# Second attention: scores and projections share one ring of five PSUM banks

## The chip, the cores and the metric
One core of a Trainium2 chip runs the whole kernel. The metric is the device time of one execution in microseconds (us). TensorE multiplies and transposes into PSUM, which has eight banks of 128 x 512 float32; VectorE and ScalarE read PSUM; GpSimd (POOL) works in SBUF; all DMAs are issued on SyncE's queue (SP).

## The reference
A decoder trunk of two layers over 2048 positions of width 1024. Each layer adds `W_out(mixer(RMSNorm(x)) * silu(gate))` to x. Layer 0 mixes by stick-breaking attention, 16 heads of 64. Layer 1, which the change touches, is multi-head latent attention with 8 heads:
```
q = rms_norm(rms_norm(q_lat) @ w_uq)          # per head 128 plain + 64 rotary
k = rms_norm(concat(kv_lat' @ w_ukv[:128], k_pe));  v = kv_lat' @ w_ukv[128:]
q, k = rope on their last 64
o = causal softmax(q k^T / sqrt(192)) v
x = x + (o * silu(gate)) @ w_out
```

## The kernel before
The program is written as a list of operations for a planner (`Sched`) inside the kernel. It gives each operation an estimated duration and issues, step by step, the one that can start first on its engine; among those that can start within 60 ns of each other, the one written first goes. So the order on each engine is fixed when the kernel is built. A matrix product of float32 quality is three products of a high and a low part (`HLS`), each a matmul of the type float32r.

A tile belongs to a ring, named by its tag, of so many buffers. A tile takes a buffer when the first operation on it is issued. A ring's queue holds its tiles in the order in which they are written. The tile at the head may take any free buffer; a tile behind the head may take one only where the ring has a `spare` number, and that many free buffers must be left over.

All PSUM comes from one pool `ps` (`bank`): three banks for `z`, two for `t`, one for `av`, two for `pj` with one spare.

The second attention goes through 32 stages (head h, group j of 512 positions). `proj1(n+1)` is written ahead of `attn1(n)`.
- `proj1` loads the latents (`ckv`, `cqt`), projects keys and values (`wukv`, two banks, the first stage `z`, the others `pj`), for every even head projects the queries of two heads (`wuq`, four banks), normalises, turns `qs`, `kn` and `kq` through one bank each, and copies half of the rotary operand `qpt` by DMA. It uses `pj`; in the first two stages also `z` and `t`.
- `attn1` makes the scores, 4(j+1) tiles `z` of five matmuls each. VectorE takes the maximum, ScalarE the exponent into `s` (a ring of 21), which releases the bank. POOL scales `s`. TensorE turns `s` through `t`, ScalarE and VectorE split it into `pt`, and three matmuls for each block add it into `av`.

Before this stage the gate of layer 1 runs through `t` and `pj` in turn (line 872). After it `out_proj` forms 16 tiles of the output, each with two accumulators, from `pj` and `z` in turn.

Of the kernel before, what the change touches and what calls it, by code (L numbers as in the profile page):

```python
# [11 lines left out]
F32 = mybir.dt.float32  # L12
# [5 lines left out]
PSUM = bass.MemoryType.PSUM  # L18
DRAM = bass.MemoryType.DRAM

P = 128
D = 1024
KD = D // P
EPS = 1e-6
NEG = -1.0e30
G = 512
# [358 lines left out]
def trunk(ctx: ExitStack, tc: tile.TileContext, x, w0, wo0, g0, g1, wlat, wgate, gqa, gkva,  # L385
# [3 lines left out]
    NT = S // P  # L389
    NG = S // G  # L390
    ctx.enter_context(tc.manual_schedule())
    sched = Sched()
# [6 lines left out]
    ps = sched.pool(lambda: tc.tile_pool(name="ps", bufs=1, space=PSUM))  # L399
    dram = ctx.enter_context(tc.tile_pool(name="dram", bufs=1, space=DRAM))  # L400

    def scratch(shape, name):
        return Buf(shape, tile=dram.tile(shape, F32, name=name))

    def bank(tag):
        bufs, spare = {"z": (3, None), "t": (2, 1), "av": (1, None), "pj": (2, 1)}[tag]
        return ps.tile([P, G], F32, tag, bufs, spare)
# [283 lines left out]
    yts = {}  # L691
# [24 lines left out]
            sched.spread(late, len(sched.ops), len(sched.ops), len(sched.ops) + 60)  # L716


    def out_proj(i, yt, xt, after=None, order=range(KD), dst=None):

        acc = [bank("pj" if i % 2 == 0 else "z") for _ in range(2)]

        def mul(ns, k):
            for a, b in HLS:
                for n in ns:
                    y = yt[k][a] if isinstance(yt[k], list) else yt[k][:, a, :]
                    w = wo[k][b][n] if isinstance(wo[k], list) else wo[k][:, b, n * G:(n + 1) * G]
                    C.mm(acc[n], y[:, i * P:(i + 1) * P], w, k == order[0] and a == 0 and b == 0,
                         k == order[-1] and a == 1)

        for ns in ((0,), (1,)) if dst is not None else ((0, 1),):
            for k in order:
                with sched.group():
                    mul(ns, k)
                if after:
                    after(k)
            for n in ns:
                cs = slice(n * G, (n + 1) * G)
                C.tt("dve", xt[:, cs], acc[n], xt[:, cs], ALU.add)
                if dst is not None:  # L740
                    C.dma(dst[:, cs], xt[:, cs], 256)
# [50 lines left out]
    for j in range(NG):  # L792
        done = []
        for i in range(4):
            t = 4 * j + i
# [128 lines left out]
    def proj1(n):  # L924
        h, j = stages[n]
        if j == 0:
            load_wh(h)
        load_c(n)
        wq, wkv = wh["q"], wh["kv"]
        kn = pa1.tile([P, 4, P], F32, "kn")  # L930
        vv = pk1.tile([P, 4, 2, P], F32R, "vv1", 6)
        ssk = pa1.tile([P, 4], F32, "ssk", 2)
        ckv = wh["ckv"]
        for i2 in range(0, 4, 2):
            acc = bank("z" if n == 0 else "pj")
            for i in range(i2, i2 + 2):
                t = slice(i * P, (i + 1) * P)
                o = 256 * (i - i2)
                with sched.group():
                    for n_, (a, b) in enumerate(HLS):  # L940
                        C.mm(acc[:, o:o + 256], ckv[:, a, t], wkv[:, b, :], n_ == 0, n_ == 2, 256)
                j1 = pa1.tile([P, QK1], BF16, "j1", 2)
                C.act(j1[:, 0:P], acc[:, o:o + P], AF.Square, P, accum=ssk[:, i:i + 1])
            av_ = acc.all().rearrange("p (i e d) -> p i e d", i=2, e=2)
            C.copy("dve", kn[:, i2:i2 + 2, :], av_[:, :, 0, :], 256)
            split(vv[:, i2:i2 + 2, 0, :], vv[:, i2:i2 + 2, 1, :], av_[:, :, 1, :], 256)
        C.tt("pool", ssk, ssk, kss[:, 4 * j:4 * j + 4], ALU.add, 4)
        rk4 = rstd(pa1, ssk, 4, QK1, "ak")
        for i in range(4):
            C.ts("dve", kn[:, i, :], kn[:, i, :], rk4[:, i:i + 1], 1.0, n=P)  # L950
        if h % 2 == 0:
            cqt = wh["cq"]
            ssq = pa1.tile([P, 8], F32, "ssq", 2)
            for i in range(4):
                acc = bank("z" if i % 2 == n else "pj")
                t = slice(i * P, (i + 1) * P)
                with sched.group():
                    for n_, (m, (a, b)) in enumerate([(m, ab) for m in range(2) for ab in HLS]):
                        C.mm(acc[:, 0:2 * QK1], cqt[:, m, a, t], wq[:, b, m, :], n_ == 0, n_ == 5, 2 * QK1)
                for e in range(2):  # L960
                    if i == 0:
                        qs1[h + e, j] = [pw1.tile([P, 4, QK1], F32, f"qs{e}", 1 + 3 * e)]
                    es = slice(e * QK1, (e + 1) * QK1)
                    j1 = pa1.tile([P, QK1], BF16, "j1", 2)
                    C.act(j1, acc[:, es], AF.Square, QK1, accum=ssq[:, 4 * e + i:4 * e + i + 1])
                    C.act(qs1[h + e, j][0][:, i, :], acc[:, es], AF.Copy, QK1)
            rq8 = rstd(pa1, ssq, 8, QK1, "aq", 5)
            for e in range(2):
                qs1[h + e, j].append(rq8[:, 4 * e:4 * e + 4])
        qs, rq4 = qs1[h, j]  # L970
        for i in range(4):
            C.ts("dve", qs[:, i, :], qs[:, i, :], rq4[:, i:i + 1], ISQ, n=QK1)
        js = slice(4 * j, 4 * j + 4)
        t1, t2 = rope(pa1, qs[:, :, P:QK1], cq[:, js, :], sq[:, js, :], 4, "rq")
        kq = pa1.tile([P, 4, 2, 64], F32, "kq")
        C.tt("pool", kq[:, :, 0, :], kper[:, js, :], rk4.all().unsqueeze(2).broadcast_to([P, 4, 64]), ALU.mult, 256)
        C.tt("pool", kq[:, :, 1, :], t1, t2, ALU.add, 256)
        qn = pk1.tile([P, 2, G], F32R, "qn", 2)
        qpt = pk1.tile([P, 2, G], F32R, "qpt", 2)
        knt = pk1.tile([P, 2, G], F32R, "knt", 5)  # L980
        kpt = pk1.tile([P, G], F32R, "kpt", 5)

        def tr(f):
            tb = bank("t" if n < 2 else "pj")
            with sched.group():
                for i in range(4):
                    C.turn(tb[:, i * P:(i + 1) * P], f(i), ident)
            return tb

        tb = tr(lambda i: qs[:, i, 0:P])  # L990
        split(qn[:, 0, :], qn[:, 1, :], tb)
        tb = tr(lambda i: kn[:, i, :])
        split(knt[:, 0, :], knt[:, 1, :], tb, gain=gqk)
        tb = tr(lambda i: kq[:, i].rearrange("p a b -> p (a b)"))
        split(kpt[0:64, :], kpt[64:128, :], tb[0:64, :])
        split(qpt[64:128, 0, :], qpt[64:128, 1, :], tb[64:128, :])
        C.dma(qpt[0:64].bitcast(F32), qpt[64:128].bitcast(F32), 256)
        kv1[h, j] = (knt, kpt, vv)
        cur1[h, j] = (qn, qpt)

    def attn1(h, j):
# [3 lines left out]
        for rt in range(4):  # L1005
# [3 lines left out]
            for g in range(j + 1):  # L1009
                knt, kpt, _ = kv1[h, g]  # L1010
                diag = g == j
                W = (rt + 1) * P if diag else G
                z = bank("z")
                with sched.group():
                    C.mm(z[:, :W], qn[:, 0, t], knt[:, 0, :W], True, False, W)
                    C.mm(z[:, :W], qn[:, 0, t], knt[:, 1, :W], False, False, W)
                    C.mm(z[:, :W], qn[:, 1, t], knt[:, 0, :W], False, False, W)
                    C.mm(z[:, :W], qpt[:, 0, t], kpt[:, :W], False, False, W)
                    C.mm(z[:, :W], qpt[:, 1, t], kpt[:, :W], False, True, W)
                if diag:  # L1020
                    C.mask_min(z[:, :W], z[:, :W], mask1[:, G - W:G], nm[:, g:g + 1], W)
                else:
                    C.reduce(nm[:, g:g + 1], z[:, :W], ALU.max, W, negate=True)
                s = pa1.tile([P, G], F32, "s", SB)
                C.act(s[:, :W], z[:, :W], AF.Exp, W, bias=nm[:, g:g + 1], scale=-1.0 if diag else 1.0,
                      accum=sm[:, g:g + 1])
                st[rt, g] = (s, W)
# [12 lines left out]
                C.ts(eng, s[:, :W], s[:, :W], c[:, g:g + 1] if j else 1.0, ri[:, 1:2], n=W)  # L1040
        g1t = pa1.tile([P, G], F32, "g1t", 2)
        C.dma(g1t, g1_d[j, h], 256)
        av = bank("av")
        for g in range(j + 1):
            vv = kv1[h, g][2]
            for c in range(4):
                r0 = c if g == j else 0
                t0 = r0 * P
                tb = bank("z" if last and c % 2 else "t")
                with sched.group():  # L1050
                    for rt in range(r0, 4):
                        C.turn(tb[:, rt * P:(rt + 1) * P], st[rt, g][0][:, c * P:(c + 1) * P], ident)
# [21 lines left out]
    yts = {}  # L1074
# [16 lines left out]
    for j in range(NG):  # L1091
        for i in range(4):
            t = 4 * j + i
            xt = pfo.tile([P, D], F32, "xr", 5)
            C.dma(xt, x1_d[t], 512)

            def ahead(k):
                if i == 1 and j + 1 < NG:
                    yts[j + 1, k] = load_y(pfo, y1_d, j + 1, k, "y", 12)

            end = out[t * P:(t + 1) * P, :]
            out_proj(i, [yts[j, k] for k in range(KD)], xt, ahead, dst=end if t == NT - 1 else None)
            if t < NT - 1:
                C.dma(end, xt, 512)

# [56 lines left out]
```

## Time and profile before
| what | us |
|---|---|
| median of 3 runs | 3049.11 (3048.87 to 3050.19) |
| the profiled execution, its own time | 3047.57 |
| its span | 3045.8 |
| TensorE busy | 2971.5 (98%) |
| VectorE busy | 2024.4 (66%) |
| ScalarE busy | 1864.7 (61%) |
| POOL busy | 1493.3 (49%) |

Busy time of TensorE counts each matmul to a modelled end, and one begins before the one ahead of it has ended. So gaps are read from the start times, and from the waits that the profile names.

### The profile page before, as it was taken

To read this page: it belongs to the slowest core of one execution; us is meant where nothing else is said; L and a number is where in the kernel's file an instruction comes from. 1 tells how busy PE (TensorE), PEld (TensorE's weight loads), DVE (VectorE), ACT (ScalarE), POOL (GpSimd) and SP (SyncE) were. 2 spreads that over 40 slices of the span, in tenths; PEclk is the share of its full clock that TensorE was granted. 3 is DMA by queue.
4 is the path that set the end of the run, shared out by engine and by line. 5 is a ranking of instruction groups with operands and counts; after the bars stand their busy time and mean duration, and the time that the engine had idled before them with its cause. 6 is when DMAs were issued, how large, how long until landed. Compare 5 with 4: busy or idle time off the path is not lost.

```text
span 3045.8 us, 48516 instructions
## 1 busy us (share of the span) xinstructions
PE 2971.5 (98%) x15728; PEld 2482.4 (82%) x15728; DVE 2024.4 (66%) x3553; ACT 1864.7 (61%) x4635; POOL 1493.3 (49%) x2931
## 2 busy tenths in 40 slices
PE   8999999999999999999999999999999999999999
PEld 6788888888888888888778888878888888888787
DVE  5787787878878788796953221147778777778511
ACT  5686776867768687786852132157776776777400
POOL 5574765756557475664652121136455555455200
PEclk9999999999999999999999999999999999999999
DMA  7434424334243343333348672142222232223462
GB/s 256 159 104 139 152 84 148 110 118 153 92 144 126 115 146 106 122 129 125 106 151 319 244 257 104 73 159 80 79 94 71 88 103 69 73 77 94 165 216 104
DMA packets 134797, 399.87 MB, mean 131 GB/s; under 512 B 16656, under 2 KB 39696, under 8 KB 131984
## 3 DMA queue, kind: packets, MB, share of 16 engines
q1 hardware_dynamic: 134544, 396.76, 38.3%
q8 instruction: 126, 2.06, 0.3%
q14 instruction: 127, 1.04, 0.1%
HBM read 272.97 MB, written 98.57 MB: 122 GB/s over the span
## 4 chain that ended last, share of the span: by engine, by line
PE 77%; DVE 11%; ACT 6%; issue 3%; POOL 2%; DMA 1%; POOLq 0%; DVEq 0%; ACTq 0%; SPq 0%
PE pj L297 30%; PE z L297 21%; PE av L297 12%; PE t L301 10%; PE t L297 3%; DVE pp L342 3%; DVE at L319 1%; DVE pt L319 1%; PE pj L301 1%; ACT s L312 1%; ACT a L312 1%; DVE qs L329 1%; DVE nm L349 1%; DVE y L319 1%; ACT z L312 1%
## 5 line engine op out<-in xcount | busy, mean ns | idle before, releaser
L297 PE MATMUL pj<-xn,w 128*128 128x512 f32 x3072 | 868.4, 403 | 1.9 <-DVE qd L319 1.9
L319 POOL TENSOR_TENSOR a<-a,pp 128x512 f32<-128x512 f32 (+3 forms) x640 | 614.2, 962 | 465.5 <-DVE pp L342 429.3
L297 PEld LDWEIGHTS pj<-xn,w 128*128 128x128 f32 x3072 | 544.5, 189 | 99.2 <-issue 3.4
L342 DVE TENSOR_TENSOR_SCAN pp<-z,cy,a 128x512 f32<-128x512 f32 x384 | 484.0, 1273 | 39.8 <-ACT z L312 37.0
L312 ACT ACTIVATE at<-t 128x512 fp32r<-128x512 f32 (+3 forms) x640 | 340.8, 535 | 148.7 <-PE t L301 146.3
L319 DVE TENSOR_TENSOR at<-t,at 128x512 fp32r<-128x512 f32 (+3 forms) x640 | 377.8, 599 | 81.0 <-ACT at L312 75.6
L312 ACT ACTIVATE a<-z 128x512 f32<-128x512 f32 (+3 forms) x640 | 335.7, 535 | 113.6 <-PE z L297 93.2
L297 PE MATMUL z<-ks,qd 128*128 128x512 f32 (+3 forms) x1280 | 362.1, 374 | 12.6 <-DVE pp L342 9.0
L297 PE MATMUL av<-at,vv 128*128 128x512 f32 (+3 forms) x1280 | 374.2, 377 | 0.2 <-DVE at L319 0.2
L301 PE MATMUL t<-ident,a 128*128 128x128 f32 x2176 | 341.4, 272 | 3.5 <-DVE at L319 1.8
L312 ACT ACTIVATE z<-z 128x512 f32<-128x512 f32 (+3 forms) x640 | 339.0, 537 | 0.8
L301 PEld LDWEIGHTS t<-ident,a 128*128 128x128 f32 x2176 | 270.9, 140 | 76.4 <-POOL a L319 2.9
L329 POOL TENSOR_SCALAR s<-s,c,ri 128x512 f32<-128x512 f32 (+3 forms) x280 | 201.0, 730 | 172.4 <-DVE ri L360 127.6
L297 PEld LDWEIGHTS z<-ks,qd 128*128 128x128 f32 x1280 | 223.3, 188 | 63.4 <-DVE pp L342 20.0
L297 PE MATMUL av<-pt,vv 128*128 128x512 f32 (+2 forms) x960 | 266.3, 384 | 5.0 <-DVE pt L319 4.2
L297 PE MATMUL z<-knt,qn 128*128 128x512 f32 (+2 forms) x960 | 256.7, 376 | 12.1 <-ACT s L312 11.9
L312 ACT ACTIVATE s<-z,nm 128x512 f32<-128x512 f32 (+2 forms) x320 | 199.9, 627 | 103.7 <-DVE nm L349 68.8
L297 PEld LDWEIGHTS av<-at,vv 128*128 128x128 f32 x1280 | 222.8, 189 | 36.3 <-DVE at L319 3.0
L319 DVE TENSOR_TENSOR pt<-t,pt 128x512 fp32r<-128x512 f32 (+1 forms) x312 | 184.2, 606 | 98.7 <-ACT pt L312 96.5
L342 DVE TENSOR_TENSOR_SCAN pp<-z,later 128x128 f32<-128x128 f32 (+3 forms) x256 | 204.3, 814 | 43.8 <-ACT z L312 26.4
L312 ACT ACTIVATE pt<-t 128x512 fp32r<-128x512 f32 (+1 forms) x312 | 163.2, 536 | 72.7 <-PE t L301 70.2
L297 PEld LDWEIGHTS z<-knt,qn 128*128 128x128 f32 x960 | 160.4, 189 | 35.8 <-ACT s L312 17.9
(238 smaller groups left out, 4942.5 us busy)
## 6 DMA issues: line engine op xcount, KB each, us to landing
xn<-xn_d SPq DMA_DIRECT2D x224, 512.0 KB, 4.7
xn_d<-xn SPq DMA_DIRECT2D x64, 512.0 KB, 4.1
y_d<-yh SPq DMA_DIRECT2D x64, 512.0 KB, 2.6
y<-y_d SPq DMA_DIRECT2D x60, 512.0 KB, 5.1
qd<-qd SPq DMA_DIRECT2D x64, 256.0 KB, 3.0
xk<-xn_d SPq DMA_DIRECT2D x32, 512.0 KB, 6.3
cqt<-c_d SPq DMA_DIRECT2D x16, 1024.0 KB, 5.0
ckv<-c_d SPq DMA_DIRECT2D x32, 512.0 KB, 3.5
```

Source lines behind the costliest of these rows:

```text
L297: lambda: self.nc.tensor.matmul(R(out), lhsT=R(l), rhs=R(r), start=start, stop=stop),
L301: self.s.add("pe", 109.0, lambda: self.nc.tensor.transpose(R(out), R(src), R(ident)), refs(out), refs(src, ident))
L312: self.nc.scalar.activation(R(out), R(src), func, **kw)
L319: self.s.add(eng, ns, lambda: self.eng[eng].tensor_tensor(out=R(out), in0=R(a), in1=R(b), op=op), refs(out), refs(a, b))
L329: self.s.add(eng, ns, lambda: self.eng[eng].tensor_scalar(out=R(out), in0=R(a), scalar1=R(s1), scalar2=R(s2), op0=op0, op1=op1), refs(out) ...
L342: lambda: self.nc.vector.tensor_tensor_scan(R(out), R(a), R(b), initial=R(init), op0=ALU.mult, op1=op),
L349: lambda: self.nc.vector.tensor_reduce(out=R(out), in_=R(src), axis=AX.X, op=op, **kw),
```

## The change
The second attention and the output projection behind it get a PSUM pool `ps1` of their own, which follows `ps`. In it `z` and `pj` are one ring of five banks with two spare; `t` keeps two with one spare, `av` one. Every `bank(...)` in `proj1`, `attn1` and the last `out_proj` becomes `bank1(...)`.
```
+    ps1 = sched.pool(lambda: tc.tile_pool(name="ps1", bufs=1, space=PSUM), after=(ps,))
+
+    def bank1(tag):
+
+        bufs, spare = {"z": (5, 2), "t": (2, 1), "av": (1, None)}["z" if tag == "pj" else tag]
+        return ps1.tile([P, G], F32, "z" if tag == "pj" else tag, bufs, spare)
+
     def bank(tag):
         bufs, spare = {"z": (3, None), "t": (2, 1), "av": (1, None), "pj": (2, 1)}[tag]
...
-    def out_proj(i, yt, xt, after=None, order=range(KD), dst=None):
+    def out_proj(i, yt, xt, after=None, order=range(KD), dst=None, bk=None):
 
-        acc = [bank("pj" if i % 2 == 0 else "z") for _ in range(2)]
+        acc = [(bk or bank)("pj" if i % 2 == 0 else "z") for _ in range(2)]
...
-            acc = bank("z" if n == 0 else "pj")
+            acc = bank1("z" if n == 0 else "pj")
...
-                acc = bank("z" if i % 2 == n else "pj")
+                acc = bank1("z" if i % 2 == n else "pj")
...
-            tb = bank("t" if n < 2 else "pj")
+            tb = bank1("t" if n < 2 else "pj")
...
-                z = bank("z")
+                z = bank1("z")
...
-        av = bank("av")
+        av = bank1("av")
...
-                tb = bank("z" if last and c % 2 else "t")
+                tb = bank1("z" if last and c % 2 else "t")
...
-            out_proj(i, [yts[j, k] for k in range(KD)], xt, ahead, dst=end if t == NT - 1 else None)
+            out_proj(i, [yts[j, k] for k in range(KD)], xt, ahead, dst=end if t == NT - 1 else None, bk=bank1)
```

## Rows read from the trace of the kernel before

**Rows 1.** The page: span, TensorE's busy time, and the chain by engine.
```profile
span 3045.8 us, 48516 instructions
...
PE 2971.5 (98%) x15728; PEld 2482.4 (82%) x15728; DVE 2024.4 (66%) x3553; ACT 1864.7 (61%) x4635; POOL 1493.3 (49%) x2931
...
PE 77%; DVE 11%; ACT 6%; issue 3%; POOL 2%; DMA 1%; POOLq 0%; DVEq 0%; ACTq 0%; SPq 0%
```

**Rows 2.** Windows: length; busy time (instructions) of five engines; TensorE's clock; DMA share; GB/s.
```profile
2019.00:2860.00 841.00, 807.05 (x4734) 696.37 (x4735) 648.01 (x1730) 606.04 (x1920) 440.88 (x647) 1.00 0.27 84
...
2860.00:3046.00 186.00, 182.17 (x800) 148.00 (x798) 26.64 (x43) 5.61 (x11) 3.86 (x3) 1.00 0.52 184
...
2025.00:2030.00 5.00, 5.00 (x25) 4.90 (x25) 3.14 (x9) 2.47 (x11) 3.04 (x5) 0.75 0.10 39
```

**Rows 3.** Waits of TensorE from 2019 to 2860 us: total, times, longest.
```profile
PE z L297 <- ACT s L312: 11.9, 18, 1.4
```

**Rows 4.** Timeline of TensorE, start of the stage: start, length, operation, [idle before <-releaser].
```profile
2019.52 0.97 PE L297 MATMUL pj<-wukv,ckv 128*128 128x256 f32 x6 [0.57 <-ACT qs L312]
...
2035.77 1.29 PE L297 MATMUL pj<-wuq,cqt 128*128 128x384 f32 x6 [1.96 <-DVE vv L319]
...
2045.45 1.33 PE L297 MATMUL pj<-wuq,cqt 128*128 128x384 f32 x6 [1.07 <-ACT qs L312]
```

**Rows 5.** Timeline of TensorE, later waits: first, the longest projection's, and last.
```profile
2081.05 0.96 PE L297 MATMUL z<-knt,qn 128*128 128x512 f32 x3 [0.90 <-ACT s L312]
...
2341.16 0.98 PE L297 MATMUL pj<-wukv,ckv 128*128 128x256 f32 x6 [0.80 <-DVE knt L336]
...
2646.04 2.33 PE L297 MATMUL pj<-wuq,cqt 128*128 128x384 f32 x12 [0.27 <-DVE ri L360]
```

**Rows 6.** Timeline of TensorE from 2470 to 2480 us.
```profile
2470.53 0.95 PE L297 MATMUL z<-knt,qn 128*128 128x512 f32 x3
...
2472.96 0.66 PE L301 MATMUL pj<-ident,kq 128*128 128x128 f32 x4 [0.43 <-POOL kq L319]
2473.84 0.96 PE L297 MATMUL z<-knt,qn 128*128 128x512 f32 x3 [0.22 <-ACT s L312]
...
2475.10 0.88 PE L297 MATMUL pj<-wukv,ckv 128*128 128x256 f32 x6
2477.41 0.79 PE L297 MATMUL z<-knt,qn 128*128 128x384 f32 x3 [1.44 <-ACT s L312]
...
2478.39 0.86 PE L297 MATMUL z<-knt,qn 128*128 128x512 f32 x3
...
2479.54 0.86 PE L297 MATMUL z<-knt,qn 128*128 128x512 f32 x3
```

**Rows 7.** Timeline of TensorE, from the last gate to the first projection.
```profile
2010.02 0.51 PE L297 MATMUL z<-wukv,ckv 128*128 128x256 f32 x3
2010.37 0.86 PE L297 MATMUL t<-xk,wgs 128*128 128x512 f32 x3
...
2013.51 0.86 PE L297 MATMUL t<-xk,wgs 128*128 128x512 f32 x3
2014.20 1.20 PE L297 MATMUL z<-wuq,cqt 128*128 128x384 f32 x6
```

**Rows 8.** Timeline of ScalarE and of VectorE at the same place.
```profile
2014.40 0.60 ACT L312 ACTIVATE sg<-t 128x512 f32<-128x512 f32 x1 [4.27 <-PE t L297]
2015.44 0.55 ACT L312 ACTIVATE qs<-z 128x192 f32<-128x192 f32 x2 [0.44 <-PE z L297]
...
2015.04 0.69 DVE L319 TENSOR_TENSOR sg<-t,sg 128x512 f32<-128x512 f32 x1 [4.18 <-ACT sg L312]
```

**Rows 9.** Timeline: a rotary DMA's issue, and the first score that needs it.
```profile
2506.72 0.47 SPq L377 DMA_DIRECT2D qpt<-qpt  x1
...
2511.90 0.96 PE L297 MATMUL z<-knt,qn 128*128 128x512 f32 x3
```

**Rows 10.** DMA issues from 1990 to 2060 us: count, KB each, median us to landing.
```profile
qpt<-qpt SPq DMA_DIRECT2D x3, 256.0 KB, 2.9
```

## The prediction, made before the change was built

> **What bounds the kernel now.** I read the page first: its span and busy lines say that TensorE is busy for 98% of 3045.8 us, and that the chain of work that ended last runs through TensorE for 77% [rows 1]. So the whole kernel hangs on TensorE's own work, and an edit to PSUM can only remove or add idle time of that engine. Next I cut the span into stretches: the second attention, from 2019 to 2860 us, holds 807.05 us of matmul in 841.00, so 34 us of idle, at a granted clock of full speed; the output projection after it is 182.17 of 186.00, and nearly all of the rest is the tail [rows 2]. The change cannot touch what comes before 2010 us except by the order in which the pools follow each other. Its field is these 34 us, about 1.1% of the kernel.
>
> Then I read what TensorE waits for in that stretch: the largest entry is the score tile `z` waiting for the exponent of an earlier score on ScalarE, 11.9 us in 18 waits [rows 3]. These are waits for a free bank. So are the waits of a projection (`pj`) for the last reader of an earlier one. The rest (the transposed weights `pt`, the rotary key `kq`, DMAs) are waits for data, which no ring of banks shortens.
>
> The question that decides is asked wait by wait in the timeline: **while TensorE waited for a bank of one ring, was one of the other ring free?** I followed each bank from its first matmul to its last reader.
> - At the start of the stage there are six, from 2019.52 to 2045.45, of 0.57 to 1.96 us [rows 4]; with the three between those shown (0.71, 0.80, 0.88) they make 6.0 us. Five are projections that wait while at least one bank of `z` is empty.
> - Later I find eleven such waits, from 2081.05 (0.90) to 2646.04 (0.27), 5.35 us together [rows 5]. At 2341.16, for one, the next key/value projection waits 0.80 us because both `pj` banks hold transposes, while the four scores of that stage are issued and one `z` bank is empty.
> - The longest repeated wait is of the other kind. The score at 2477.41 waits 1.44 us with three scores in their banks (the first and the last of them at 2470.53 and 2473.84), the transposed `kq` and a key/value projection in the other two [rows 6]: five of five are taken. Waits of that kind sum to 8.6 us (twelve of them). There VectorE and ScalarE are late, and one ring of five has no bank more than three and two.
>
> **The change, part by part.**
>
> *One ring of five in place of three and two.* Ceiling: 6.0 + 5.35 = 11.35 us of named idle in 17 waits. Each wait costs slightly more than its name: before 2477.41 the six projection matmuls begun at 2475.10 need 6 x 0.117 = 0.70 us (0.117 from the step of three such matmuls, 2010.02 to 2010.37 [rows 7]), so the gap is 1.61 us, not 1.44; that is 0.17 each, 2.9 us for 17. Ceiling 14.2 us, floor nothing. What is late next when such a stall goes: the readers. A score issued earlier meets VectorE and ScalarE at the work that kept them, so some of the idle comes back a few matmuls later. Since 8.6 of the 20 us of bank waits are already of the kind where the readers are late, I let a third come back: gain 9.5 us.
>
> *The spare rule.* Before, a score may take any of three banks and a projection out of turn needs both of its two free. After, a tile that is not at the head of the common queue needs three free banks, so while the next projection is still waiting for its data, scores and other projections together hold three banks; before it was three plus one. Once the projections of a stage have their banks, the scores are the head and may take all five. Cost of the first between nothing (TensorE fills in with transposes and value matmuls, which keep their own three banks) and one score of 1.15 us (its five matmuls, from 2478.39 to 2479.54 [rows 6]) in each of the 16 stages that project queries, 18 us. I take 1 us, near the lower end, because value matmuls lie ready in those stretches.
>
> *A pool of its own.* The new pool opens only when every tile of the old one has been released, the last by the gate of the last group. Before, four key/value groups of the first stage slip between the last gate's matmuls, the first at 2010.02, and the query projection follows at 2014.20 [rows 7]. After, they queue behind the gate: the gate's last matmuls end 4 x 0.35 = 1.4 us earlier, at about 2013.0 (from 2013.51 + 0.86 less 1.4), then sigmoid 0.60 and product 0.69 [rows 8] release its bank at about 2014.3. TensorE stands idle for some 1.4 us and then runs the four groups; the query projection starts at 2015.75 instead of 2014.20. What hides it: ScalarE, which in the old order first reads a projection at 2015.44 [rows 8] and is then busy without a break until 2023; it gets its first key/value group at about 2014.9 in the new order, no later than before. Bounds: 0, and 1.55 us plus a spell at the lower clock. The row of 2025 to 2030 shows such a spell, a granted clock of 0.75 of full speed (1.2 GHz for half of it) after the waits before it [rows 2]; at half speed for 2.5 us it costs up to 1.25 us. I take 1 us of 0 to 2.8. No DMA is added; the loads of `ckv` and `cqt` on SP's queue keep their order.
>
> *Output projection.* Its two accumulators come from the ring of five in place of two rings in turn. TensorE has no gap there to lose [rows 2]; cost nothing, covered by the matmuls of the next pair of accumulators, 186 / 16 = 11.6 us; were the cover gone, each of 16 pairs would wait for one pass of VectorE over a bank, 0.69 us as the product in [rows 8], 11 us in all. The same tiles in the last attention: the transposes that borrow `z` banks have five to borrow from; nothing.
>
> **Sum.** -9.5 + 1 + 1 = -7.5 us. The profiled execution took 3047.57 us (span 3045.8 and 1.8 around it), so 3040.1 by its own time; it lies 1.5 below the median of the runs, so against the median 3049.1 - 7.5 = 3041.6.
>
> **The rivals.**
>
> *The scores hog the ring (slower).* While scores are at the head they may fill all five banks; the projection of the stage after next, which had two banks of its own, then starts behind them. TensorE takes its matmuls in program order, so a score that waits holds the projection behind it as well: at 2477.41 nothing else ran. The Trainium skill says the same ("PSUM — Partial Sum Buffer", section "Engine vs sequencer instructions": matmuls start and complete in program order), and the trace agrees with that wait of 1.44 us. How much delay is free: the DMA that completes the rotary operand is issued at 2506.72 and lands 2.9 us later, at 2509.6, and the first score that needs it starts at 2511.90 [rows 9, 10], a slack of 2.3 us. Two scores put ahead (2.3 us) are just free; three (3.45 us) cost 1.15 us in each stage. Over the 16 stages with twelve or more scores, which can fill the ring, and without the gain of the first part: 3049.1 + 18 + 2 = 3069; with the gain, 3060. For it: the chain from projection to rotary operand lasts some 27 us and ends that close to its use. Against: value matmuls of the stage before fill in. It decides from three scores on.
>
> *Nothing comes of it.* All removed idle returns, since VectorE (77% busy in this stretch by 648.01 of 841.00 [rows 2]) and ScalarE were what banks waited for: 3049.1 + 0 to 2, so 3050. For it: the wait at 2477.41 with all five taken.
>
> *All bank waits go.* The order that the planner writes with a common ring also moves the scores away from the moments when readers are late: 11.35 + 8.6 us and 0.17 for each of 29 waits, 25 us, less 2: 3026. The Trainium skill ("Perfetto Trace Analysis", section "Optimization Strategy") holds that the same gap repeating on the engine that should be saturated can mean that there is not enough PSUM for the next tile. The trace bears that out in the waits of [rows 5] and not in that of [rows 6], where the readers, not the split of the banks, set the release.
>
> **How the numbers follow.** A measurement of this kernel can tell about 0.2%, 6 us, from no change. Forecast (a gain of about 4 to 13 us): 0.40; all waits gone: 0.07; nothing, within 6 us either way: 0.29; slower by the hogged ring: 0.24. Of the forecast a little lies inside 6 us, of "nothing" a little outside it on the gain's side, about as much. So faster 0.47, same 0.29, slower 0.24. The range runs from 3028, nearly all waits gone, to 3060, the hogged ring with its gain; one tenth is left out at either end. The forecast's own range is 3036 to 3046.
>
> **What would show it.** Right: in the second attention the idle of TensorE falls from 34 to some 26 us; "z waits for s" falls from 11.9 to about 8 and the projections' waits at the start nearly vanish; the waits with five banks taken stay. At the boundary the key/value groups of stage one come after the last gate with a gap of about 1.4 us. Wrong: new waits for the rotary DMA or for `kq` ahead of scores mean a hogged ring; a longer stretch from 2010 to 2060, or a clock below full speed there, means that the pool's boundary costs more than ScalarE hides. The planner writes another order of instructions for the whole stage from its own estimates of their durations, so waits for data can come or go that no row here foretells; that is what would most easily upset the sum.

## The result, and the profile after

| | us |
|---|---|
| before, median of 6 runs | 3048.89 (3045.99 to 3050.19) |
| after, median of 6 runs | 3026.49 (3025.70 to 3028.95) |
| ratio after / before, 95% interval | 0.9927 [0.9917, 0.9938] |

The kernel becomes faster by 22.4 us. The direction was forecast; the size (7.5) is three times too small, and the time lies 1.5 us below the range, where the rival "all bank waits go" had put it.

The page of the kernel after, beside [rows 1]: the span is 18.6 us shorter, and TensorE's share of the chain that ended last rises from 77 to 79%.
```profile
span 3027.2 us, 48544 instructions
...
PE 79%; DVE 10%; ACT 6%; issue 2%; DMA 2%; POOL 1%; SPq 0%; DVEq 0%; ACTq 0%; POOLq 0%
```
A window of the kernel after, beside [rows 2]: TensorE's idle in it is 841.00 - 823.50 = 17.5 us, against 34 before and 26 forecast.
```profile
2019.00:2860.00 841.00, 823.50 (x4847) 713.22 (x4846) 652.45 (x1742) 610.55 (x1946) 446.46 (x652) 1.00 0.29 91
```
Waits of TensorE from 2019 to 2860 us, after (total, times, longest). The entry of [rows 3], a score that waits for an exponent to free a bank, falls from 11.9 us in 18 waits to 1.9 in 2. The largest is now a value matmul that waits for transposed weights, which is a wait for data.
```profile
PE av L297 <- DVE pt L319: 5.3, 18, 0.7
PE t L301 <- DVE qs L329: 4.1, 2, 2.1
PE z L297 <- ACT s L312: 1.9, 2, 1.1
```

**Where the time came from.** The second attention can be cut in every kernel at the same three events, read in one execution of each: the end of the last gate matmuls, the first product `y` of head 1 (stage (1, 0)), and the last `y` (stage (7, 3)). So head 0 is one phase, "start", and heads 1 to 7 are another, "rest". VectorE's timeline gives the two products, before:
```profile
2160.99 0.68 DVE L319 TENSOR_TENSOR y<-av,g1t 128x512 f32<-128x512 f32 x1
...
2873.17 0.69 DVE L319 TENSOR_TENSOR y<-av,g1t 128x512 f32<-128x512 f32 x1 [1.88 <-PE av L297]
```
and after:
```profile
2164.26 0.69 DVE L319 TENSOR_TENSOR y<-av,g1t 128x512 f32<-128x512 f32 x1
...
2854.57 0.69 DVE L319 TENSOR_TENSOR y<-av,g1t 128x512 f32<-128x512 f32 x1 [0.53 <-PE av L297]
```
The gate ends at 2013.51 + 0.86 = 2014.37 before [rows 7] and at 2011.84 + 3.56 = 2015.40 after (the boundary's rows, below). So:
- start: 2160.99 - 2014.37 = 146.6 before, 2164.26 - 2015.40 = 148.9 after: 2.2 us **longer**.
- rest: 2873.17 - 2160.99 = 712.2 before, 2854.57 - 2164.26 = 690.3 after: 21.9 us **shorter**.
- from the last `y` to the end of the span: 172.6 in both, so the output projection gave and took nothing.

With 1.0 us that the gate ended later, 1.0 + 2.2 - 21.9 = -18.7, the difference of the two spans to the rounding. The execution of after that was profiled took 3028.95 us, the longest of its six, which is why the medians differ by more. It was late before the change could act: TensorE's order is the same in both kernels up to one group of gate matmuls, which starts at 2009.34 before (below) and at 2011.84 after.
```profile
2009.34 0.84 PE L297 MATMUL t<-xk,wgs 128*128 128x512 f32 x3
```
The cuts don't hold quite the same work, so the idle of TensorE says more than a length. Windows of the start and of the rest, before and then after:
```profile
2014.37:2160.99 146.62, 134.73 (x788) 115.70 (x788) 111.49 (x304) 107.18 (x362) 80.04 (x123) 0.99 0.32 98
2160.99:2873.17 712.18, 689.89 (x4039) 595.40 (x4038) 543.96 (x1441) 507.89 (x1587) 364.65 (x528) 1.00 0.27 85
```
```profile
2015.40:2164.26 148.86, 136.89 (x811) 119.49 (x811) 113.62 (x312) 108.35 (x372) 81.26 (x125) 0.99 0.31 96
2164.26:2854.57 690.31, 683.38 (x4026) 591.58 (x4027) 539.58 (x1432) 502.85 (x1579) 363.92 (x526) 1.00 0.28 88
```
The start has 23 matmuls more after than before (12 of them are the four key/value groups that ran ahead of the gate's end before [rows 7]) and the same idle, 11.9 and 12.0 us: it neither gained nor lost. In the rest the idle falls from 22.3 to 6.9 us. The whole gain lies in heads 1 to 7, where the work repeats every two heads.

**One period of two heads**, from the `y` of stage (3, 0) to that of (5, 0): the same 1200 matmuls by the records. Windows of before, then of after: 210.70 us becomes 203.90, TensorE's idle 7.3 becomes 1.9.
```profile
2371.90:2582.60 210.70, 203.39 (x1200) 176.15 (x1200) 161.89 (x434) 152.25 (x486) 110.84 (x165) 1.00 0.26 83
```
```profile
2369.20:2573.10 203.90, 202.04 (x1200) 175.65 (x1200) 160.15 (x433) 150.49 (x486) 110.58 (x164) 1.00 0.27 86
```
The waits of TensorE in these two windows; before they sum to 7.2 us in 16 (with three not shown, of 0.3, 0.2 and 0.2):
```profile
PE z L297 <- ACT s L312: 3.1, 5, 1.4
PE av L297 <- DVE pt L319: 1.2, 4, 0.5
PE pj L301 <- POOL kq L319: 0.8, 2, 0.4
PE pj L297 <- DVE knt L336: 0.8, 1, 0.8
PE pj L297 <- DVE nm L355: 0.6, 1, 0.6
```
and after, all that are named, 1.7 us in 7:
```profile
PE av L297 <- DVE pt L319: 1.3, 5, 0.4
PE t L301 <- DVE pt L319: 0.2, 1, 0.2
PE z L297 <- ACT j L312: 0.2, 1, 0.2
```
Not only the waits where a bank of the other ring was free are gone. So are the 1.44 us of [rows 6], where five of five were taken, and two waits for the rotary key `kq`, which were waits for data. The timeline of TensorE shows how: the planner's order is another one. Before, the projections of one stage are cut into pieces as `pj` banks come free, with scores between them (first and last: 2394.50 to 2409.17).
```profile
2394.50 1.60 PE L297 MATMUL pj<-wukv,ckv 128*128 128x256 f32 x12
...
2398.23 1.22 PE L297 MATMUL pj<-wuq,cqt 128*128 128x384 f32 x6
...
2407.88 1.29 PE L297 MATMUL pj<-wuq,cqt 128*128 128x384 f32 x6
```
After, the same 36 matmuls run nearly in one go, from 2391.23 to 2397.87: two key/value and three query banks, and the fourth query bank after eight transposes.
```profile
2391.23 1.60 PE L297 MATMUL z<-wukv,ckv 128*128 128x256 f32 x12
2392.66 3.29 PE L297 MATMUL z<-wuq,cqt 128*128 128x384 f32 x18
2395.79 1.04 PE L301 MATMUL t<-ident,s 128*128 128x128 f32 x8
2396.58 1.29 PE L297 MATMUL z<-wuq,cqt 128*128 128x384 f32 x6
```
And at the place in the period that had the wait of 1.44 us, eight scores run without a wait (the first at 2464.58, the last at 2472.96) and the projections follow behind them all, where before a key/value projection stood ahead of the score that waited.
```profile
2471.06 0.86 PE L297 MATMUL z<-knt,qn 128*128 128x512 f32 x3
...
2472.96 0.94 PE L297 MATMUL z<-knt,qn 128*128 128x512 f32 x3
...
2474.19 1.64 PE L297 MATMUL z<-wukv,ckv 128*128 128x256 f32 x12
```
ScalarE's timeline shows what this order does for the readers. Before, the score begun at 2470.53 [rows 6] keeps its bank until its exponent ends at 2477.27, for 6.7 us: ScalarE takes parts of the rotary operands first, and waits for VectorE between them.
```profile
2475.96 0.59 ACT L312 ACTIVATE qpt<-pj 64x512 fp32r<-64x512 f32 x1 [0.73 <-DVE kpt L319]
2476.58 0.69 ACT L312 ACTIVATE s<-z,nm 128x512 f32<-128x512 f32 x1
```
After, the same score begins at 2466.29 and its exponent (timeline of ScalarE, after) ends at 2470.32: 4.0 us.
```profile
2469.63 0.69 ACT L312 ACTIVATE s<-z,nm 128x512 f32<-128x512 f32 x1
```
Over heads 1 to 7, with each score's first matmul matched to its exponent by width and order, 22 of 268 scores keep their bank for more than 5.2 us before, the longest for 7.5; after, none does (the longest 5.0).

**The boundary**, timeline of TensorE and then of ScalarE, beside [rows 7] and [rows 8]: the key/value groups stand behind the gate, after a gap of 1.41 us (1.4 was forecast), and ScalarE reads the first projection at 2017.82.
```profile
2011.84 3.56 PE L297 MATMUL t<-xk,wgs 128*128 128x512 f32 x15
2016.81 1.69 PE L297 MATMUL z<-wukv,ckv 128*128 128x256 f32 x12 [1.41 <-DVE sg L319]
```
```profile
2017.82 0.28 ACT L312 ACTIVATE j<-z 128x128 bf16<-128x128 f32 x1 [1.79 <-PE z L297]
```

### The profile page after: what moved, and what is told of

The parts are those of the page before. It is cut to its first block, busy times and chain, and to the rows that moved or that the text cites. A ratio compares the mean times of both kernels' runs of the same rounds, so it can differ in the third digit from the quotient of the medians.

```text
span 3027.2 us, 48544 instructions
## 1 busy us (share of the span) xinstructions
PE 2966.1 (98%) x15728; PEld 2481.1 (82%) x15728; DVE 2023.9 (67%) x3553; ACT 1861.2 (61%) x4635; POOL 1493.6 (49%) x2931
## 3 DMA queue, kind: packets, MB, share of 16 engines
q14 instruction: 127, 1.04, 0.1%
## 4 chain that ended last, share of the span: by engine, by line
PE 79%; DVE 10%; ACT 6%; issue 2%; DMA 2%; POOL 1%; SPq 0%; DVEq 0%; ACTq 0%; POOLq 0%
PE z L297 28%; PE pj L297 25%; PE av L297 12%; PE t L301 10%; PE t L297 3%; DVE pp L342 3%; DVE at L319 1%; DVE pt L319 1%; ACT a L312 1%; DVE qs L329 1%; PE z L301 1%; DVE nm L349 1%; ACT s L312 1%; DVE y L319 1%; ACT j L312 1%
## 5 line engine op out<-in xcount | busy, mean ns | idle before, releaser
L297 PE MATMUL z<-ks,qd 128*128 128x512 f32 (+3 forms) x1280 | 363.3, 375 | 13.2 <-DVE pp L342 10.3
L297 PEld LDWEIGHTS av<-at,vv 128*128 128x128 f32 x1280 | 222.7, 189 | 36.4 <-DVE at L319 3.3
L297 PEld LDWEIGHTS av<-pt,vv 128*128 128x128 f32 x960 | 159.6, 189 | 32.0 <-DVE pt L319 15.1
```

The source lines that it names most:

```text
L297: lambda: self.nc.tensor.matmul(R(out), lhsT=R(l), rhs=R(r), start=start, stop=stop),
```

## The experiments

The theory after the result: what counts is that one bank can serve either kind at the time of its burst, so that the planner writes another order. The rivals: scores gained because they may hold more banks than three; any freedom to go out of turn would do; or the new pool itself, with its new order of the start, moved the time.

Each ratio is to the kernel before on the same chip (medians 3048.89 to 3050.19 there). "Start" and "rest" are the phases above, read in each kernel's trace in the same way and given as the difference from before.

| kernel | median us | ratio [95%] | start | rest |
|---|---|---|---|---|
| after | 3026.49 | 0.9927 [0.9917, 0.9938] | +2.2 | -21.9 |
| own pool, rings of before | 3062.71 | 1.0044 [1.0031, 1.0057] | +13.3 | -0.6 |
| the same, scores may go out of turn | 3061.25 | 1.0038 [1.0026, 1.0051] | +17.5 | +0.7 |
| two rings, `z` 2 and `pj` 3 | 3058.71 | 1.0032 [1.0019, 1.0044] | +9.4 | -2.0 |
| ring of five, scores at most three | 3036.72 | 0.9956 [0.9943, 0.9968] | +4.9 | -18.6 |
| ring of five, projections at most two | 3049.60 | 0.9998 [0.9989, 1.0007] | +13.2 | -13.8 |
| ring of five, projections at most three | 3036.06 | 0.9963 [0.9949, 0.9976] | +4.8 | -14.9 |
| ring of five, one spare | 3027.46 | 0.9927 [0.9915, 0.9940] | +1.9 | -22.3 |
| ring of five, three spare | 3058.20 | 1.0029 [1.0018, 1.0040] | +6.9 | +5.5 |
| ring of five, in written order | 3132.85 | 1.0272 [1.0258, 1.0286] | +13.9 | +71.8 |
| pool opened tile by tile | 3027.26 | 0.9923 [0.9909, 0.9936] | -0.8 | -21.9 |
| one pool, ring of five in both attentions | 3225.53 | 1.0576 [1.0561, 1.0591] | +2.6 | -22.9 |
| ring of seven (with `t`) | 3022.77 | 0.9912 [0.9898, 0.9925] | -7.9 | -19.6 |

Two cautions on the last two columns. A few us there can be work that lies on the other side of a cut: the start holds from 765 matmuls (ring of seven) to 833 (scores at most three), and the time behind the last `y` is 3.4 to 3.6 us longer than before with `z` 2 and `pj` 3, projections at most two, one spare and the ring of seven (1.4 or less in the others). And the start can hold stretches at the lower clock: TensorE's granted clock over it is 0.99 of full speed before and after, but 0.97 with the pool alone, 0.95 with projections at most two and 0.93 where scores may go out of turn.

**The pool alone.** The own pool, with the rings of before in it.
```
-        bufs, spare = {"z": (5, 2), "t": (2, 1), "av": (1, None)}["z" if tag == "pj" else tag]
-        return ps1.tile([P, G], F32, "z" if tag == "pj" else tag, bufs, spare)
+        bufs, spare = {"z": (3, None), "t": (2, 1), "av": (1, None), "pj": (2, 1)}[tag]
+        return ps1.tile([P, G], F32, tag, bufs, spare)
```


> Pool of its own, but the rings as before (z three, pj two with one spare). If the whole gain comes from the common ring, this is the cost of the boundary alone: 3049 to 3052 us by the prediction's own term (0 to 2.8, taken as 1). If the new pool's place in the order is what helps, it comes near 3026.

It is slower than before by 12.5 us, outside what was expected, and by its trace all of it at the start; the rest is unchanged. So the ring is worth not 22 but some 36 us (3062.71 to 3026.49); the two traces, of the shortest execution here and the longest of after, place 11 of them at the start and 21 in the rest. The loss is not at the boundary's gap, which is 1.41 us here too. Most of it falls some 80 us later, in the third stage (from `y` to `y` 44.4 us, 36.4 before), where two projection banks make TensorE wait for a chain of VectorE (timeline of TensorE in this kernel):
```profile
2097.70 0.63 PE L301 MATMUL pj<-ident,kq 128*128 128x128 f32 x4 [1.38 <-DVE qn L319]
...
2101.16 0.94 PE L297 MATMUL pj<-wukv,ckv 128*128 128x256 f32 x6 [1.92 <-DVE qpt L319]
```

**Order without more banks.** The same, with `z` allowed out of turn.
```
-        bufs, spare = {"z": (3, None), "t": (2, 1), "av": (1, None), "pj": (2, 1)}[tag]
+        bufs, spare = {"z": (3, 1), "t": (2, 1), "av": (1, None), "pj": (2, 1)}[tag]
```


> As e1 (own pool, rings of three and two), but scores may be taken out of turn with one bank left over; in the old ring of three they could not. Theory O (what the common ring gives is freedom of order, not banks): well under e1, 3035 to 3050. Theory of banks (it gives banks to whoever needs them): as e1, 3058 to 3066.

The rest stays at +0.7: freedom of order for the scores alone gives nothing.

**The other fixed split.** One bank goes from scores to projections.
```
-        bufs, spare = {"z": (3, None), "t": (2, 1), "av": (1, None), "pj": (2, 1)}[tag]
+        bufs, spare = {"z": (2, None), "t": (2, 1), "av": (1, None), "pj": (3, 1)}[tag]
```


> Two rings again, split the other way: scores two banks, projections three. Theory P: a part of the gain remains, 3035 to 3046, since three banks make a shorter burst than five. Theory S: slower than before, over 3055, since scores lose one of three banks and wait for their readers on each tile.

Still slower than before; the rest gains 2.0 and the time behind it loses 3.5. It is not that projections had too few banks in the mean: what they gain the scores lose, which now wait for an exponent 10.0 us in 23 waits over the rest (9.3 in 14 before).

**The common ring with one kind held down.** The planner counts the banks that each kind holds. Scores (all tiles with the tag `z`, so some projections of the first two stages, the odd accumulators of the output projection and the borrowed transposes too) hold at most three:
```
+    cap1 = [0.0] * 3
...
+        b.cap = cap1 if tag == "z" else None
...
+                            t = max(t, sorted(b.cap)[m - 1])
```


> Ring of five with the same spare rule, but scores (all tiles asked for as z) may hold at most three banks at once; projections may hold all five. Theory P (the gain is that projections run in one burst and their data is ready early): 3026 to 3031. Theory S (the gain is that scores run up to five deep and ride over late readers): 3043 to 3051, no better than before.

The time lies between the two theories. Of the 21.3 us that the ring takes out of the rest (-0.6 to -21.9) this keeps 18.0, though scores have no bank more than before; of the idle that goes there (22.9 us with the pool alone, 6.9 after) it keeps away 13.2. The waits of TensorE in its period of two heads, from 2369.2 to 2574.8 us, name no score that waits for an exponent at all:
```profile
PE av L309 <- DVE pt L331: 1.6, 4, 0.9
PE z L313 <- DVE qs L341: 0.2, 1, 0.2
PE z L309 <- ACT j L324: 0.2, 1, 0.2
PE t L313 <- DVE pt L331: 0.2, 1, 0.2
```
So those waits were not for want of a score bank. The long holds are gone too: no score keeps its bank for more than 5.2 us (with the pool alone 22 do, the longest for 7.4). The same with projections held at two (out of turn only when another is left):
```
+    cap1 = [0.0] * 2
...
+        b.cap = cap1 if tag == "pj" else None
```


> Ring of five with the same spare rule, but projections may hold at most two banks at once, out of turn only where one more is left, as before; scores may hold all five. Theory P: 3043 to 3051. Theory S: 3026 to 3031. If both kinds need the extra banks at different times, e2 and e3 both land between, 3032 to 3042.

It keeps 13.2 of the 21.3 us in the rest (8.9 us by idle), but all of the loss at the start, and comes out as before. Here 14 scores still keep a bank for more than 5.2 us, the longest for 7.5, so what it keeps is not that readers come sooner: with up to five banks, fewer scores have to wait for them. With three banks for projections:
```
-    cap1 = [0.0] * 2
+    cap1 = [0.0] * 3
```


> As e3, but projections may hold three banks at once, out of turn only where one more is left. If what counts is how many banks a projection's burst may fill, between e3 and the changed kernel, 3032 to 3042; if two were too few only because a turned tile waiting for its readers blocks one, three are enough: 3025 to 3031.

The start falls from +13.2 to +4.8, the rest from -13.8 to -14.9. So at the start it is the third projection bank that counts, by its waits and by the clock: the start's idle falls from 17.0 to 12.4 us, and its granted clock rises from 0.95 to 0.99 of full speed. In the rest either freedom, scores up to five or projections up to five, brings more than half of the gain by itself, and the two overlap (18.0 + 13.2 against 21.3).

**The reserve.** Spare of one, three and none, where two is the change's.
```
-        bufs, spare = {"z": (5, 2), "t": (2, 1), "av": (1, None)}["z" if tag == "pj" else tag]
+        bufs, spare = {"z": (5, 1), "t": (2, 1), "av": (1, None)}["z" if tag == "pj" else tag]
```


> The changed kernel with one spare bank instead of two: tiles behind the head may hold four banks. The prediction's term for the spare rule was a cost of 1 us (0 to 18); by it this is the changed kernel or up to some us faster, 3020 to 3027. Rival, the hogged ring: with one spare the scores leave too little for the next projection, 3035 or more.

No difference from after that the runs can tell: the second spare bank costs nothing.
```
-        bufs, spare = {"z": (5, 2), "t": (2, 1), "av": (1, None)}["z" if tag == "pj" else tag]
+        bufs, spare = {"z": (5, 3), "t": (2, 1), "av": (1, None)}["z" if tag == "pj" else tag]
```


> The changed kernel with three spare banks: tiles behind the head may hold two. If scores seldom need more than two while a projection is pending (the prediction's reason for 1 us), within 5 us of the changed kernel, 3023 to 3032. If the spare banks are a price in earnest, 3035 to 3050.

The third costs 31 us, which neither reading of the rule had expected, and makes the ring slower than the kernel before, about as slow as two rings in a pool of their own.
```
-        bufs, spare = {"z": (5, 2), "t": (2, 1), "av": (1, None)}["z" if tag == "pj" else tag]
+        bufs, spare = {"z": (5, None), "t": (2, 1), "av": (1, None)}["z" if tag == "pj" else tag]
```


> The changed kernel, with the common ring taken strictly in the order written. Scores written behind a projection then wait for it to begin. If freedom of order matters in a common ring (three spare banks cost 31 us over two), far slower than the changed kernel, over 3060; if not, 3026 to 3040.

In the order written the ring costs 106 us against after. What is held up is the chain from projection to scores: the longest waits of TensorE from 2060 to 2840 us in this kernel are for weights, a turn of the queries, and what follows from them.
```profile
PE t L301 <- POOL s L329: 21.9, 11, 2.1
PE av L297 <- DVE pt L319: 11.4, 25, 1.0
PE z L301 <- DVE qs L329: 10.3, 3, 3.4
```
They are only part of it. The window of the rest has 784.01 - 729.56 = 54.5 us of idle (6.9 in after), and a granted clock of 0.96 of full speed:
```profile
2172.49:2956.50 784.01, 729.56 (x4059) 617.89 (x4058) 567.99 (x1460) 515.78 (x1602) 366.51 (x532) 0.96 0.25 77
```
By the mean clock of the profiled executions (0.986 over 3130.5 us, 0.998 over 3027.2) some 38 of the 106 us are the lower clock, an estimate that takes TensorE as busy all through the slow stretches.

**The boundary's gap.** The new pool takes each bank over when the tile in that bank is released, not when all are.
```
-    ps1 = sched.pool(lambda: tc.tile_pool(name="ps1", bufs=1, space=PSUM), after=(ps,))
+    ps1 = sched.pool(lambda: tc.tile_pool(name="ps1", bufs=1, space=PSUM, reuse_waits="tile"), after=(ps,))
```


> The changed kernel, with the new pool's banks waiting each for the old tiles in that bank only, not for the whole old pool; the planner's order is the same. The wait of 1.4 us for the gate's product ahead of the first key/value projection shrinks or goes. If the boundary's price is that wait, 1 to 2 us faster than the changed kernel; if ScalarE sets the start of the stage, as the prediction took it, no difference.

The gap is gone (timeline of TensorE in this kernel):
```profile
2012.73 3.56 PE L297 MATMUL t<-xk,wgs 128*128 128x512 f32 x15
2016.13 1.59 PE L297 MATMUL z<-wukv,ckv 128*128 128x256 f32 x12
```
TensorE's order is that of after. In the trace its start is 3.0 us shorter than that of after, 1.8 of it idle, the rest a granted clock of 1.00 in place of 0.99; but the medians can't tell the two (3027.26 and 3026.49). Whether the gap is worth anything is open.

**Without a pool of its own.** Before, with the ring of five in the one pool, so in the first attention and the other products too.
```
-        bufs, spare = {"z": (3, None), "t": (2, 1), "av": (1, None), "pj": (2, 1)}[tag]
-        return ps.tile([P, G], F32, tag, bufs, spare)
+        bufs, spare = {"z": (5, 2), "t": (2, 1), "av": (1, None)}["z" if tag == "pj" else tag]
+        return ps.tile([P, G], F32, "z" if tag == "pj" else tag, bufs, spare)
```


> No pool of its own: the kernel before, with one ring of five (two spare) for scores and projections in the whole kernel, the first attention too. If the boundary is what the change still pays (e1 was 12 us slower than before), the second attention starts earlier and the whole is 3014 to 3026. If the boundary costs nothing once the ring is common, the second attention is as in the changed kernel and only the first attention can move the time; its bank waits (z for the scan's last reader, 10.9 us in 21 waits) bound the gain: 3010 to 3035.

The second attention gains what it gains in after (rest -22.9, start +2.6 without any boundary), and the work ahead of it loses 195 us (the gate ends at 2208.70 + 0.86 = 2209.56, against 2014.37), where a gain had been expected. The largest entry among the waits of TensorE from 0 to 1700 us in this kernel: scores of the first attention wait for VectorE's scan `pp`, 48.1 us where the same view of before has 10.0.
```profile
PE z L297 <- DVE pp L342: 48.1, 96, 1.2
```
Part of the 195 us is again the clock: 0.98 of full speed up to the gate's end, 1.00 before. The own pool is what keeps the ring out of there.

**A wider ring.** Projections, scores and the turns `t` from one ring of seven.
```
-        bufs, spare = {"z": (5, 2), "t": (2, 1), "av": (1, None)}["z" if tag == "pj" else tag]
-        return ps1.tile([P, G], F32, "z" if tag == "pj" else tag, bufs, spare)
+        bufs, spare = {"z": (7, 2), "av": (1, None)}["av" if tag == "av" else "z"]
+        return ps1.tile([P, G], F32, "av" if tag == "av" else "z", bufs, spare)
```


> The changed kernel, with the turned tiles t in the common ring too: seven banks with two spare, and one av. If the remaining idle (value matmuls waiting for pt, 5.3 us in 18 waits) is for want of banks for turned tiles, 3018 to 3026; if it waits for VectorE and ScalarE, no difference, 3023 to 3031; if turned tiles of long life crowd out the projections, 3035 or more.

It has the lowest median of all, 3.7 us under after, but the intervals of the two ratios overlap. Where a gain would come from is not shown: its start is shorter (-7.9 against +2.2) but holds 46 matmuls fewer than that of after, the rest and the time behind it are longer, and TensorE's idle in both phases is 20.6 us, against 18.9 in after.

## Why the prediction was right in sign and short in size

- **The view was right.** TensorE's idle in the second attention was the whole field: the gain came from there, and from no other part (the tail is 172.6 us in both); the idle in the two phases fell from 34.2 to 18.9 us.
- **The term that failed is the ring's -9.5 us, and the step in it "waits of that kind ... one ring of five has no bank more than three and two".** Forecast at -7.5 with the other terms, the two phases measured -19.6 (-21.9 in the rest), and -32 against the pool alone. The waits with five of five taken went as well, and with scores held at their old three banks they were still gone. The snapshot of banks at the wait was correct as read, but it was taken in an order that the two rings had produced. With a common ring the planner puts the projections of a stage elsewhere and closer together, and the bank that was full at 2477.41 is not asked for at that moment. The readers were late because of that order: before, 22 scores keep a bank for more than 5.2 us, after none, and the waits for `kq` and `knt` vanish too. That the planner's new order, and not some other consequence of the ring, moves the readers is read from the timelines at one place of the period and argued for the others.
- **"A third comes back" failed with it.** In the period of two heads, 5.4 of the 7.3 us of idle stay away; the next waits (`av` for `pt`) kept their 1.2 to 1.3 us.
- **The place was wrong too.** Of the 11.35 us of named idle 6.0 lay at the start [rows 4]. They did not turn into time: TensorE now waits there for the turned queries (4.1 us) and at the boundary (1.4) instead of for `pj` banks; from 2010 to 2060 us the waits named sum to 8.1 us before and 8.2 after, and the start's idle is 11.9 and 12.0. The gain is where only 5.35 us had been named [rows 5].
- **Spare and boundary, +2 us together,** look like the start's +2.2, but that is luck: the +2.2 is work on the other side of the cut. The boundary's order came as forecast: a gap of 1.41 us, and, less the 2.5 us that this execution was late before it, the query projection at 2015.84 (2015.75 forecast; 2018.34 in the trace). What it costs no run isolates. The spare rule cost nothing against one spare. And the bound of 2.8 us for the pool held only together with the ring: with the old rings the pool costs 13, by a way that the prediction did not see (two projection banks, 80 us behind the boundary).
- **0.17 us on top of each wait's name** held in the period: a period has nine waits fewer (16 to 7), 5.5 us by name, 1.5 more by that rule, 7.0, and is 6.8 shorter.
- **Rivals.** Scores that hog the ring were not seen: no wait for the rotary DMA entered the list, and a lower cap on scores made the kernel slower. "Nothing comes of it" fell with the same step as the forecast. "All bank waits go" named the mechanism that the runs bear out, an order that moves the scores away from late readers, and had a chance of 0.07. That its time was right to a microsecond is in part luck: its arithmetic counted the start's 6.0 us too, which did not come, while waits for data went that it did not count.

## What to carry to other kernels

Where a planner writes the order, a count of free banks at the moment of a wait says what that order needed, not what another split would need: ask which burst of work the split cuts into pieces. Two kinds of tiles with bursts at different times share one ring well if a tile behind the head may pass and a small reserve stays for the head (here one or two of five; with three the gain was gone, and strict order made it far slower). Give such a ring a pool of its own where another stage of the kernel would lose by it, and try that pool alone first, because its price can hide in the gain.

## What the runs showed of the hardware that was not expected

In the kernel with the pool alone, TensorE worked 3.36 of 7.00 us from 2095 on, and in the next four microseconds its granted clock was 0.60 of full speed, so a mix of 1.2 and 2.4 GHz (windows of that kernel):
```profile
2095.00:2102.00 7.00, 3.36 (x22) 2.38 (x20) 5.57 (x18) 5.05 (x16) 5.73 (x10) 1.00 0.00 1
2102.00:2106.00 4.00, 3.90 (x18) 3.43 (x18) 2.30 (x5) 2.16 (x7) 3.83 (x8) 0.60 0.72 199
```
Its timeline shows what that cost: eight transposes took 1.80 us, against 1.04 at 2395.79 in after, and three score matmuls 1.63 against 0.86.
```profile
2102.68 1.80 PE L301 MATMUL t<-ident,s 128*128 128x128 f32 x8
2104.12 1.63 PE L297 MATMUL z<-knt,qn 128*128 128x512 f32 x3
```
So some 1.5 us (0.76 + 0.77) at this place is not waiting but slower matmuls after the waits. In after the same stage, from 2084 to 2120 us, has one wait of 1.05 us and a granted clock of 1.00. Nor is it the only such place. The whole start of the kernel with the pool alone has 159.87 - 140.71 = 19.2 us of idle and a granted clock of 0.97:
```profile
2012.83:2172.70 159.87, 140.71 (x800) 120.43 (x801) 113.44 (x304) 108.58 (x362) 80.02 (x123) 0.97 0.29 90
```
Before, the start has 11.9 us of idle and 0.99. So of the 13.3 us some 7 are idle, 1.4 are the key/value groups that lie behind the cut here, and about 3 are the lower clock (0.02 of 160 us). So a kernel that waits more can lose again by the clock, here about 3 us and some 38 with the ring in written order; that the waits came first is seen only at the place above.
